# A two-layer hybrid decoder trunk: small matmuls on one pool of four PSUM banks, and another order of the first weights

## The chip, the cores and the metric

One core of a Trainium2 chip. The metric is the device time of one execution in microseconds, as the median of several runs; lower is better.

## What is computed

256 positions of width 1024 pass through two layers. A layer first runs three token mixers beside each other on one combined projection, merges them by gates, projects and adds; then it runs a SwiGLU feed-forward part. All arrays are float32.

```python
for l in range(DEPTH):                                   # 2
    h = _rmsnorm(x, mix_norm[l])
    proj = (h @ w_in[l]).astype(jnp.float32)             # 1024 x 5892
    ret_c, fox_c, rwkv_c, gate_c = jnp.split(proj, splits, axis=-1)
    y_ret = _retention_branch(ret_c, ...)                # 4 heads of 64, masked scores
    y_fox = _fox_branch(fox_c, ...)                      # 4 heads of 64, softmax with forget gates
    y_rwkv = _rwkv7_branch(rwkv_c, ...)                  # 4 heads of 64, recurrent state
    gates = jax.nn.sigmoid(gate_c).reshape(B, S, 3, D)
    merged = (gates[:, :, 0] * (y_ret @ p_ret[l]) + gates[:, :, 1] * (y_fox @ p_fox[l])
              + gates[:, :, 2] * (y_rwkv @ p_rwkv[l]))
    x = x + merged @ w_out[l]
    h = _rmsnorm(x, ffn_norm[l])
    g, u = jnp.split(h @ w_gate_up[l], 2, axis=-1)       # 2 x 2816
    x = x + (jax.nn.silu(g) * u) @ w_down[l]
```

## The kernel before

**Large products.** Activations lie transposed, features on the partitions, as eight tiles of 128 by 256. Every float32 operand of a large product is split into a high and a low part of type fp32r, and a product is three matmuls: high by high, then the two mixed ones (`mm3`, line 300). Weights come by DMA as pieces of 1 MB into three `raw` buffers, ACT casts the high part of eight tiles (line 287), DVE subtracts for the low part (288); four such pairs (`whi`, `wlo`) are buffered, and `refill` (294) keeps up to three cast pieces ahead. The products of one pair of output tiles collect in one PSUM bank of the tag "mm" (four banks). `gemm_n` (489) makes the columns of fox and ret that are needed with the positions on the partitions.

**Small products.** The mixers use about a thousand matmul records with few rows, columns or both. RWKV's go to two PSUM banks of the tag "rw", those of fox, ret and the norms to two of the tag "fr". Many address a part of the array: 64 rows by 128 columns (`pgm` 807, `psc` 1183, one head of a pair in each half of the rows), 128 by 64 (`pyf` 1123, `pyr` 1191, `pU` 947, the first part of `py` 972), 64 by 64 (`pn` 887 and 894, `pm` 859, `par` 935, `pS` 957, the second part of `py` 980), 32 by 32 (`px` 906 and 914) and 128 by 8 (`pc` 1061, the running sums of the forget gates). Transposes (`ptr` 842, `pqk`, `px` 1113, `pv` 998) use the whole array. `pb` (793) is the bonus product of RWKV; DVE reads it for `bon` (795). In `fox` the causal mask is added by a bf16 product of an identity with the mask, behind the diagonal block's scores (1101).

**Order.** `mixers` (539) runs generators: the large products ("gemm") and the chains of RWKV, fox and ret. Each `yield` gives a cost from the table `PACE`, and the generator whose clock is lowest goes next; where the merge needs a branch (`self.need`), that one runs to its end first. This gives every instruction a rank, and the framework's scheduler then orders each engine's instructions by rank and by estimated times of readiness, allots buffers and sets the waits. On the chip each engine keeps that order.

**The start.** 22 products of zeros run first (`pz`, 172 to 176). The first weight tile `w[0]` is fetched in three pieces: columns 0 to 511 on ACT's queue, 512 to 1023 and 1024 to 2047 on SP's queue, which also fetches x, the parameters and the next tiles, in the order of lines 183 to 191. `first_pairs` (345) goes over the contraction in four steps of two feature tiles, and in each over four pairs of outputs; a pair and step has four weight tiles, hence twelve matmuls, tile by tile through `mm3`. In its last step come the sums of squares and `replicate` (474), which puts the inverse norm on all partitions for `rwkv_in` (672).

## Time and profile before

| | |
|---|---|
| runs | 795.17, 795.45, 798.04 us; median 795.45 |
| the profiled execution | 795.98 us, its span 794.0 us |
| TensorE (PE) | 785.9 us busy, 99% |
| VectorE (DVE) | 569.4 us, 72% |
| ScalarE (ACT) | 403.6 us, 51% |
| GpSimd (POOL) | 15.0 us, 2% |
| DMA | 140.42 MB, mean 177 GB/s |
| granted clock of TensorE | 1.0 |

The span runs from the first to the last instruction of the profiled execution; its own time has 2.0 us more. All stretches are in microseconds from the span's start. Layer 0's mixers lie between about 31 and 185 us, its feed-forward part ends near 410, and layer 1 follows in the same shape. PE is matmul and PEld the weight load that overlaps it; a matmul record lasts longer than the distance to the next one, since matmuls are pipelined. One float32 matmul of the program leaves two records.

### The profile page before, as it was taken

The numbers are of one execution on the slowest core, as the hardware profiler recorded it, in microseconds if no ns is written. First come the engines' busy times: TensorE is split into PE (matmuls) and PEld (weight loads), VectorE is DVE, ScalarE is ACT, GpSimd is POOL, SyncE is SP. The second block draws the span as 40 slices with busy tenths as digits, with TensorE's granted clock in tenths as the row PEclk, the third lists the DMA queues.
The fourth block names the chain that finished last, engine by engine and source line by source line (L and its number), as shares of the span: only waits on it lengthen the run. The fifth ranks groups of instructions, "written<-read, shape, count | busy, mean of one in ns | idle before, by whom it ended". The sixth has DMA issues, their size and how long they took to land.

```text
span 794.0 us, 16539 instructions
## 1 busy us (share of the span) xinstructions
PE 785.9 (99%) x7010; PEld 761.8 (96%) x7010; DVE 569.4 (72%) x919; ACT 403.6 (51%) x563; POOL 15.0 (2%) x51
## 2 busy tenths in 40 slices
PE   8999999999999999999999999999999999999998
PEld 7999999999999999999998998998999999999998
DVE  5887888778866666656668798877787766666453
ACT  6577445345646544535446773544356544444331
POOL 3000000000000000000020000000000000000000
PEclk9999999999999999999999999999999999999999
DMA  8755434425555555555564453442355465564650
GB/s 319 259 173 181 152 118 167 133 74 220 192 193 201 178 206 193 171 195 199 199 203 174 174 173 111 167 166 81 134 213 211 161 213 176 196 210 162 208 192 27
DMA packets 28234, 140.42 MB, mean 177 GB/s; under 512 B 7648, under 2 KB 9216, under 8 KB 13184
## 3 DMA queue, kind: packets, MB, share of 16 engines
q1 hardware_dynamic: 28016, 139.10, 50.5%
q8 instruction: 55, 0.90, 0.5%
q10 hardware_dynamic: 144, 0.26, 0.1%
q14 instruction: 19, 0.16, 0.1%
HBM read 136.97 MB, written 1.33 MB: 174 GB/s over the span
## 4 chain that ended last, share of the span: by engine, by line
PE 94%; DVE 2%; DMA 2%; ACT 1%; issue 0%; SPq 0%; DVEq 0%; ACTq 0%
PE mm L304 27%; PE mm L307 27%; PE mm L308 27%; DVE wlo L288 1%; PE mqk L487 1%; PE mqk L486 1%; PE mqk L485 1%; DMA raw<-in_win 1%; ACT whi L287 1%; PE mv L485 1%; PE pgm L807 1%; PE mv L486 1%; PE mv L487 1%; DMA rsw<-rqk 1%; PE ptr L842 1%; PE psc L1183 0%
## 5 line engine op out<-in xcount | busy, mean ns | idle before, releaser
L287 ACT CAST whi<-raw 128x1024 fp32r<-128x1024 f32 (+1 forms) x257 | 264.9, 1033 | 311.4 <-PE mm L307 220.6
L288 DVE TENSOR_TENSOR wlo<-raw,whi 128x1024 fp32r<-128x1024 f32 (+1 forms) x257 | 308.7, 1203 | 152.0 <-ACT whi L287 151.4
L304 PE MATMUL mm<-xh,whi 128*128 128x256 f32 x1312 | 367.6, 280 | 1.6 <-ACT whi L287 1.3
L308 PE MATMUL mm<-xh,wlo 128*128 128x256 f32 x1264 | 351.0, 278 | 0.1
L307 PE MATMUL mm<-xl,whi 128*128 128x256 f32 x1264 | 350.6, 277 | 0.1
L304 PEld LDWEIGHTS mm<-xh,whi 128*128 128x128 f32 x1312 | 246.6, 188 | 4.0 <-ACT whi L287 1.5
L307 PEld LDWEIGHTS mm<-xl,whi 128*128 128x128 f32 x1264 | 237.5, 188 | 1.4 <-issue 0.5
L308 PEld LDWEIGHTS mm<-xh,wlo 128*128 128x128 f32 x1264 | 237.3, 188 | 1.1 <-issue 0.3
L307 PE MATMUL mm<-lo,whi 128*128 128x256 f32 x576 | 160.2, 278 | 0.2
L308 PE MATMUL mm<-hi,wlo 128*128 128x256 f32 x576 | 160.2, 278 | 0.0
L304 PE MATMUL mm<-hi,whi 128*128 128x256 f32 x576 | 160.0, 278 | 0.0
L307 PEld LDWEIGHTS mm<-lo,whi 128*128 128x128 f32 x576 | 108.2, 188 | 1.0 <-DVE lo L425 0.6
L304 PEld LDWEIGHTS mm<-hi,whi 128*128 128x128 f32 x576 | 108.2, 188 | 0.6 <-issue 0.3
L308 PEld LDWEIGHTS mm<-hi,wlo 128*128 128x128 f32 x576 | 108.1, 188 | 0.3
L650 DVE TENSOR_TENSOR h<-t,mm 128x512 f32<-128x512 f32 x22 | 15.1, 687 | 11.3 <-PE mm L308 8.4
L647 DVE TENSOR_TENSOR t<-mm,rstd 128x512 f32<-128x512 f32 (+1 forms) x24 | 15.1, 645 | 8.5 <-PE mm L308 8.5
L485 PE MATMUL mv<-whi,xh 128*128 128x260 f32 (+1 forms) x64 | 18.7, 293 | 0.0
L487 PE MATMUL mv<-whi,xl 128*128 128x260 f32 (+1 forms) x64 | 18.4, 287 | 0.0
L588 DVE TENSOR_TENSOR gate<-mm,rstd 128x512 f32<-128x512 f32 x24 | 16.4, 684 | 2.7 <-PE mm L308 2.7
L486 PE MATMUL mv<-wlo,xh 128*128 128x260 f32 (+1 forms) x64 | 18.4, 287 | 0.0
L597 DVE SCALAR_TENSOR_TENSOR gate<-gate,mm 128x512 f32<-128x512 f32 x24 | 15.9, 678 | 2.4 <-PE mm L308 2.3
L440 ACT ACTIVATE xh<-x,par 128x256 fp32r<-128x256 f32 x32 | 14.8, 501 | 2.5 <-DVE x L661 1.7
(257 smaller groups left out, 716.5 us busy)
## 6 DMA issues: line engine op xcount, KB each, us to landing
raw<-in_wg SPq DMA_DIRECT2D x44, 1024.0 KB
raw<-in_wgate SPq DMA_DIRECT2D x24, 1024.0 KB
raw<-in_wd SPq DMA_DIRECT2D x16, 1024.0 KB
raw<-in_win SPq DMA_DIRECT2D x13, 1024.0 KB
raw<-in_wo SPq DMA_DIRECT2D x8, 1024.0 KB
raw<-in_wd SPq DMA_DIRECT2D x8, 768.0 KB
raw<-in_wqk SPq DMA_DIRECT2D x4, 1024.0 KB
raw<-in_pp SPq DMA_DIRECT2D x4, 1024.0 KB
```

Of the source, the lines that this page charges most:

```text
L287: nc.scalar.copy(hi[:, :m * width], r)
L288: nc.vector.tensor_tensor(out=lo[:, :m * width], in0=r, in1=hi[:, :m * width].bitcast(F32), op=ALU.subtract)
L304: nc.tensor.matmul(out, wh, xh, start=first, stop=False)
L307: nc.tensor.matmul(out, wh, xl, start=False, stop=False)
L308: nc.tensor.matmul(out, wl, xh, start=False, stop=last)
L485: nc.tensor.matmul(out, xh[:, s], wh, start=first, stop=False)
L486: nc.tensor.matmul(out, xh[:, s], wl, start=False, stop=False)
L487: nc.tensor.matmul(out, xl[:, s], wh, start=False, stop=last)
L588: nc.vector.tensor_tensor(out=g, in0=ps, in1=self.b2(rstd), op=ALU.mult)
L597: nc.vector.scalar_tensor_tensor(out=g, in0=g, scalar=1.0, in1=ps, op0=ALU.add, op1=ALU.mult)
L647: nc.vector.tensor_tensor(out=t[:, o, :], in0=p, in1=self.bs(rstd, o), op=ALU.mult)
L650: nc.vector.tensor_tensor(out=h, in0=t, in1=pu, op=ALU.mult)
```

## The change

- **Banks.** The tags "rw" and "fr" become one tag "sm" with four banks (`SM`); "mm" keeps four. All the lines that only rename the tag are left out below.
- **The start.** The third piece of `w[0]` and the whole of `w[1]` go to ACT's queue, behind the first piece; SP keeps the rest, x's last part comes behind `w[2]`. `first_pairs` takes four weight tiles at a time and runs the four high by high products first, then the four with the low part of the weights, then those with the low part of x.
- **replicate** moves behind the first step of "gemm" in layer 0; `rstd` is handed over in a list. In layer 1 its place stays.
- **Joined groups.** In `pn` (887), both `px` (906 and 914; one shown) and `par` (935) the loop over heads or halves is reversed. The first part of `py` moves up to stand behind `pU`; the second part runs in reverse. `psc` is made for two heads at a time in two banks, with one `yield` in place of four. `pyf` and `pyr` share a new function `rows_out`, which alternates the two column halves, last operand first. `pc` gets a weight operand padded with zeros to 128 columns. The mask goes ahead of the scores, two blocks in one product.

```diff
+SM = 4
...
         nc.sync.dma_start(par[0], d["par"][0, :, 0:P_RES])
+        nc.scalar.dma_start(w[0][:, 1024:2048], d["win0"][0, :, 1024:2048])
         nc.sync.dma_start(w[0][:, 512:1024], d["win0"][0, :, 512:1024])
-        nc.sync.dma_start(w[0][:, 1024:2048], d["win0"][0, :, 1024:2048])
-        for j in range(1, 4):
-            nc.sync.dma_start(self.xt[j], d["xt"][:, 2 * j:2 * j + 2, :])
-            if j < 3:
-                nc.sync.dma_start(w[j][:, 0:2048], d["win0"][j])
+        nc.scalar.dma_start(w[1][:, 0:2048], d["win0"][1])
+        nc.sync.dma_start(self.xt[1], d["xt"][:, 2:4, :])
+        nc.sync.dma_start(self.xt[2], d["xt"][:, 4:6, :])
+        nc.sync.dma_start(w[2][:, 0:2048], d["win0"][2])
+        nc.sync.dma_start(self.xt[3], d["xt"][:, 6:8, :])
...
-        ps = [self.ps.tile([P, 2, T], F32, tag=t, bufs=n, name=self.nm("mm")) for t, n in (("rw", 2), ("rw", 2), ("mm", 4), ("mm", 4))]
+        nc = self.nc
+        ps = [self.ps.tile([P, 2, T], F32, tag=t, bufs=n, name=self.nm("mm")) for t, n in (("sm", SM), ("sm", SM), ("mm", 8 - SM), ("mm", 8 - SM))]
...
-                if kk == 3 and j == 3:
-                    rstd = self.replicate(dg)
-                for m in range(2):
-                    for k in range(2 * kk, 2 * kk + 2):
-                        if not self.cur:
-                            self.refill()
-
-                        self.mm3(ps[j][:, m, :], self.block(), xs[k], k == m == 0, k == KT - 1 and m == 1)
-        return ps, rn, rstd
+                ws = []
+                while len(ws) < 4:
+                    if not self.cur:
+                        self.refill()
+                    ws.append(self.block())
+
+                for n, (i, o) in enumerate(((0, 0), (1, 0), (0, 1))):
+                    for b in range(4):
+                        m, k = b // 2, 2 * kk + b % 2
+                        nc.tensor.matmul(ps[j][:, m, :], ws[b][i], xs[k][o], start=n == b == kk == 0, stop=n == 2 and b == 3 and kk == 3)
+        return ps, rn, dg
...
-            ps, rn, rstd = self.first_pairs(xs)
+            ps, rn, dg = self.first_pairs(xs)
...
-            rstd = self.replicate(dg)
-        rw = self.rwkv_in(l, xs, rstd, ps)
-        clock = {"gemm": 0.0, "rwkv": 0.0}
-        run = {"gemm": self.gemms(l, xs, rstd, rn), "rwkv": self.rwkv(l, rw)}
+        rstd = []
+        gemms = self.gemms(l, xs, rstd, rn)
+        clock = {"gemm": next(gemms) if l == 0 else 0.0, "rwkv": 0.0}
+        rstd.append(self.replicate(dg))
+        rw = self.rwkv_in(l, xs, rstd[0], ps)
+        run = {"gemm": gemms, "rwkv": self.rwkv(l, rw)}
...
         for p in range(NP):
-            for h in range(2):
+            for h in (1, 0):
                 nc.tensor.matmul(px[hs[h], p, :], nn[hs[h], p, :], dn[hs[h], p, :], start=True, stop=True, tile_position=(64 * h, 64 * h))
...
-        for a in range(2):
-            pa = self.ps.tile([P, NC - 1, 2 * C], F32, tag="rw", bufs=2, name=self.nm("par"))
+        for a in (1, 0):
+            pa = self.ps.tile([P, NC - 1, 2 * C], F32, tag="sm", bufs=SM, name=self.nm("par"))
...
-        pu = self.ps.tile([P, 2, NC - 1, 64], F32, tag="rw", bufs=2, name=self.nm("pU"))
+        pu = self.ps.tile([P, 2, NC - 1, 64], F32, tag="sm", bufs=SM, name=self.nm("pU"))
         for q in range(NC - 1):
             for a in range(2):
...
                     nc.tensor.matmul(pu[hs[h], a, q, :], gg[:, u, 0:C], uw[:, u, :], start=q == a == 0, stop=q == NC - 2 and a == 1,
                                      tile_position=(0, h * 64))
+
+        py = [self.ps.tile([P, 2, 2, C], F32, tag="sm", bufs=SM, name=self.nm("py")) for _ in range(2)]
+        for q2 in range(NC // 2):
+            for a in range(2):
+                for h in range(2):
+                    for e in range(2):
+                        u = unit(a, 2 * q2 + e, h)
+                        nc.tensor.matmul(py[h][hs[e], q2, a, :], gg[:, u, C:2 * C], uw[:, u, :], start=q2 == a == 0, stop=False,
+                                         tile_position=(0, e * 64))
...
-                pS = self.ps.tile([P, 64], F32, tag="rw", bufs=2, name=self.nm("pS"))
+                pS = self.ps.tile([P, 64], F32, tag="sm", bufs=SM, name=self.nm("pS"))
...
-        py = [self.ps.tile([P, 2, 2, C], F32, tag="rw", bufs=2, name=self.nm("py")) for _ in range(2)]
-        for q2 in range(NC // 2):
...
-        for q2 in range(NC // 2):
-            for a in range(2):
-                for e in range(2):
+        for q2 in (1, 0):
+            for a in (1, 0):
+                for e in (1, 0):
                     for h in range(2):
                         q = 2 * q2 + e
                         if q:
                             nc.tensor.matmul(py[h][hs[e], q2, a, :], ar[hs[h], a, q, C:], S[a][q - 1][hs[h], :], start=False,
-                                             stop=q2 == NC // 2 - 1 and a == 1, tile_position=(64 * h, e * 64))
+                                             stop=q2 == 1 - e and a == 0, tile_position=(64 * h, e * 64))
...
-        pt = lambda n, shape: self.ps.tile(shape, F32, tag="fr", bufs=2, name=self.nm(n))
-
-        na, lf = sm.tile([P, 2, 4], F32, name="na"), sm.tile([P, 2, 8], F32, name="lf")
+        pt = lambda n, shape: self.ps.tile(shape, F32, tag="sm", bufs=SM, name=self.nm(n))
+
+        na, lf = sm.tile([P, 2, 4], F32, name="na"), sm.tile([P, 2, P], F32, name="lf")
+        nc.gpsimd.memset(lf[:, :, 8:], 0.0)
...
-        nc.tensor.matmul(pc[0:8, :], lf[:, 0, :], c["tri"][:, 0, :], start=True, stop=False)
-        nc.tensor.matmul(pc[0:8, P:T], lf[:, 1, :], c["tri"][:, 1, P:T], start=False, stop=True)
+        nc.tensor.matmul(pc, lf[:, 0, :], c["tri"][:, 0, :], start=True, stop=False)
+        nc.tensor.matmul(pc[:, P:T], lf[:, 1, :], c["tri"][:, 1, P:T], start=False, stop=True)
...
                 pl = pt("pl", [P, 2, T])
+
+                nc.tensor.matmul(pl[:, :, t * P:n], self.identb, self.maskb.unsqueeze(1).broadcast_to([P, 2, P]), start=True, stop=False)
                 for i in range(2):
                     h = 2 * a + i
                     for b in range(t + 1):
-                        o = pl[:, i, b * P:(b + 1) * P]
-                        nc.tensor.matmul(o, qa[:, h, t * P:(t + 1) * P], ka[:, h, b * P:(b + 1) * P], start=True, stop=b < t)
-                        if b == t:
-                            nc.tensor.matmul(o, self.identb, self.maskb, start=False, stop=True)
+                        nc.tensor.matmul(pl[:, i, b * P:(b + 1) * P], qa[:, h, t * P:n], ka[:, h, b * P:(b + 1) * P],
+                                         start=False, stop=i == 1 and b == t)
...
-        for h in range(4):
-            a, s = h // 2, slice((h % 2) * 64, (h % 2) * 64 + 64)
-            vs = slice(h * 64, h * 64 + 64)
-            nc.tensor.matmul(py[s, a, 0:P], v[:, 0, vs], pT0[:, h, 0:P], start=True, stop=True)
-            nc.tensor.matmul(py[s, a, P:T], v[:, 0, vs], pT0[:, h, P:T], start=True, stop=False)
-            nc.tensor.matmul(py[s, a, P:T], v[:, 1, vs], pT1[:, h, :], start=False, stop=True)
+        self.rows_out(py, lambda t, h: v[:, t, h * 64:h * 64 + 64], pT0, pT1)
         self.dbg("fox", l, py)
         self.y[1] = self.split(self.t2, py, [P, 2, T], ("t2", "t2"))
+
+    def rows_out(self, py, v, p0, p1):
+
+        for a in (1, 0):
+            for first, t, q, p in ((True, 1, slice(P, T), p1), (False, 0, slice(P, T), p0), (True, 0, slice(0, P), p0)):
+                for i in (1, 0):
+                    h = 2 * a + i
+                    self.nc.tensor.matmul(py[i * 64:i * 64 + 64, a, q], v(t, h), p[:, h, :] if t else p[:, h, q], start=first,
+                                          stop=not first or q.start == 0)
...
-        for h in range(4):
-            a, s = h // 2, slice((h % 2) * 64, (h % 2) * 64 + 64)
-            ps = self.ps.tile([P, 384], F32, tag="fr", bufs=2, name=self.nm("psc"))
-            nc.tensor.matmul(ps[:, 0:T], qk[s, 2 + a, 0:P], qk[s, a, :], start=True, stop=True)
-            nc.tensor.matmul(ps[:, T:], qk[s, 2 + a, P:T], qk[s, a, P:T], start=True, stop=True)
-            nc.vector.tensor_tensor(out=sc[:, h, :], in0=ps[:, 0:T], in1=rmask[:, h, :], op=ALU.mult)
-            nc.vector.tensor_tensor(out=sc1[:, h, :], in0=ps[:, T:], in1=rmask[:, h, 0:P], op=ALU.mult)
-            yield PACE["ret1"]
-        py = self.ps.tile([P, 2, T], F32, tag="fr", bufs=2, name=self.nm("pyr"))
-        for h in range(4):
-            a, s = h // 2, slice((h % 2) * 64, (h % 2) * 64 + 64)
-            nc.tensor.matmul(py[s, a, 0:P], v[:, 0, h, :], sc[:, h, 0:P], start=True, stop=True)
-            nc.tensor.matmul(py[s, a, P:T], v[:, 0, h, :], sc[:, h, P:T], start=True, stop=False)
-            nc.tensor.matmul(py[s, a, P:T], v[:, 1, h, :], sc1[:, h, :], start=False, stop=True)
+        for a in range(2):
+            ps = [self.ps.tile([P, 384], F32, tag="sm", bufs=SM, name=self.nm("psc")) for _ in range(2)]
+            for t in range(2):
+                for i in range(2):
+                    s = slice(i * 64, i * 64 + 64)
+                    nc.tensor.matmul(ps[i][:, t * T:T + t * P], qk[s, 2 + a, t * P:(t + 1) * P], qk[s, a, t * P:], start=True, stop=True)
+            for i in range(2):
+                h = 2 * a + i
+                nc.vector.tensor_tensor(out=sc[:, h, :], in0=ps[i][:, 0:T], in1=rmask[:, h, :], op=ALU.mult)
+                nc.vector.tensor_tensor(out=sc1[:, h, :], in0=ps[i][:, T:], in1=rmask[:, h, 0:P], op=ALU.mult)
+        yield PACE["ret1"]
+        py = self.ps.tile([P, 2, T], F32, tag="sm", bufs=SM, name=self.nm("pyr"))
+        self.rows_out(py, lambda t, h: v[:, t, h, :], sc, sc1)
```

## Rows read from the trace of the kernel before

**Rows 1.** The page's head: span, busy time by engine, chain that ended last by engine.
```profile
span 794.0 us, 16539 instructions
...
PE 785.9 (99%) x7010; PEld 761.8 (96%) x7010; DVE 569.4 (72%) x919; ACT 403.6 (51%) x563; POOL 15.0 (2%) x51
...
PE 94%; DVE 2%; DMA 2%; ACT 1%; issue 0%; SPq 0%; DVEq 0%; ACTq 0%
```

**Rows 2.** Busy time by stretch: length, then PE, PEld, DVE, ACT, POOL, clock, DMA.
```profile
91.27:107.05 15.78, 15.75 (x142) 13.50 (x141) 13.56 (x23) 3.27 (x5) 0.00 (x0) 1.00 0.29 105
...
235.40:410.30 174.90, 174.90 (x1538) 174.87 (x1537) 110.20 (x122) 85.80 (x102) 4.29 (x12) 1.00 0.55 191
```

**Rows 3.** Timeline of PE: start, length, line, operation, tiles, shapes, matmuls merged.
```profile
91.06 0.28 PE L308 MATMUL mm<-xh,wlo 128*128 128x256 f32 x1
91.27 1.16 PE L807 MATMUL pgm<-rav,bk 64*128 64x128 f32 x8
92.35 0.39 PE L304 MATMUL mm<-xh,whi 128*128 128x256 f32 x1
92.57 0.28 PE L307 MATMUL mm<-xl,whi 128*128 128x256 f32 x1
...
101.57 0.94 PE L807 MATMUL pgm<-rav,bk 64*128 64x128 f32 x14
102.35 0.41 PE L1183 MATMUL psc<-rqk 64*128 64x256 f32 x1
```

**Rows 4.** Timelines of PE and DVE: the product pb and its reader.
```profile
83.56 1.02 PE L793 MATMUL pb<-rkk,con 128*128 128x512 f32 x2
...
98.95 0.68 DVE L795 TENSOR_TENSOR bon<-v,pb 128x512 f32<-128x512 f32 x1
```

**Rows 5.** Timeline of PE: first and last row of ptr and pyr in turn.
```profile
104.59 0.99 PE L842 MATMUL ptr<-con,rav 128*128 128x128 f32 x6
...
106.83 0.39 PE L308 MATMUL mm<-xh,wlo 128*128 128x256 f32 x1
```

**Rows 6.** Timeline of PE: two records of a group ahead of the rest.
```profile
145.84 0.33 PE L887 MATMUL pn<-dn,nn 64*64 64x64 f32 x2 [0.15 <-DVE dn L882]
146.09 0.39 PE L304 MATMUL mm<-hi,whi 128*128 128x256 f32 x1
...
153.71 0.21 PE L906 MATMUL px<-t,gg 32*32 32x32 f32 x2
153.85 0.39 PE L308 MATMUL mm<-hi,wlo 128*128 128x256 f32 x1
```

**Rows 7.** Timeline of PE: py begins, large products after it, pv.
```profile
168.31 0.69 PE L972 MATMUL py<-uw,gg 128*64 128x64 f32 x16
...
170.64 0.38 PE L304 MATMUL mm<-xh,whi 128*128 128x256 f32 x1
...
179.03 0.60 PE L998 MATMUL pv<-con,ysq 128*128 128x128 f32 x4
```

**Rows 8.** Timeline of PE: pc and the second large matmul behind it.
```profile
62.19 0.60 PE L1061 MATMUL pc<-con,lf 128*8 128x256 f32 x2
...
63.16 0.28 PE L307 MATMUL mm<-xl,whi 128*128 128x256 f32 x1
```

**Rows 9.** Timeline of the start, PE and ACT; in brackets the wait and its releaser.
```profile
6.23 0.58 PE L304 MATMUL mm<-xh,whi 128*128 128x256 f32 x1 [0.31 <-ACT xh L440]
...
7.28 0.28 PE L304 MATMUL mm<-xh,whi 128*128 128x256 f32 x1
...
8.22 0.62 ACT L287 CAST whi<-raw 128x512 fp32r<-128x512 f32 x1 [1.64 <-DMA raw<-in_win]
...
8.89 0.39 PE L304 MATMUL mm<-xh,whi 128*128 128x256 f32 x1 [1.33 <-ACT whi L287]
```

**Rows 10.** Busy time by stretch, columns as in rows 2; DMA share and GB/s end the line.
```profile
3.50:6.00 2.50, 2.43 (x12) 1.39 (x10) 0.36 (x2) 0.85 (x2) 1.77 (x6) 1.00 0.74 178
...
8.00:10.00 2.00, 1.11 (x9) 1.11 (x10) 0.69 (x1) 1.13 (x2) 0.00 (x0) 1.00 1.00 419
```

More of the change, by code (lines that the diff above doesn't have):

```diff
@@ L322, in gemm_halves @@
     def gemm_halves(self, xs, kcut=None, hook=None, tag="mm"):
-        ps = [self.ps.tile([P, T], F32, tag=tag, bufs=4 if tag == "mm" else 2, name=self.nm("mm")) for _ in range(2)]
+        ps = [self.ps.tile([P, T], F32, tag=tag, bufs=8 - SM if tag == "mm" else SM, name=self.nm("mm")) for _ in range(2)]
         n = len(xs) if kcut is None else KT
@@ L489, in gemm_n @@
     def gemm_n(self, width, xs, name="mv"):
-        ps = [self.ps.tile([P, width], F32, tag="mm", name=self.nm(name)) for _ in range(2)]
+        ps = [self.ps.tile([P, width], F32, tag="mm", bufs=8 - SM, name=self.nm(name)) for _ in range(2)]
         for k in range(KT):
@@ L543, in mixers @@
         if l == 0:
-            ps, rn, rstd = self.first_pairs(xs)
+            ps, rn, dg = self.first_pairs(xs)
         else:
-            ps = [self.gemm_halves(xs, 7, tag="rw"), self.run(self.gemm_pair(xs))]
+            ps = [self.gemm_halves(xs, 7, tag="sm"), self.run(self.gemm_pair(xs))]
             rn, dg = self.rstd()
             ps.append(self.run(self.gemm_pair(xs)))
-            rstd = self.replicate(dg)
-        rw = self.rwkv_in(l, xs, rstd, ps)
-        clock = {"gemm": 0.0, "rwkv": 0.0}
-        run = {"gemm": self.gemms(l, xs, rstd, rn), "rwkv": self.rwkv(l, rw)}
+        rstd = []
[4 more added lines that the diff above has]
+        run = {"gemm": gemms, "rwkv": self.rwkv(l, rw)}
         self.start = []
@@ L578, in gemms @@
         rt = []
-        for _ in self.ret_in(l, xs, rstd, rn, rt):
+        for _ in self.ret_in(l, xs, rstd[0], rn, rt):
             yield PACE["gemms1"]
@@ L587, in gate @@
             g = gates[b, c] = self.big.tile([P, 2, T], F32, tag="gate", bufs=8, name=self.nm("gate"))
-            nc.vector.tensor_tensor(out=g, in0=ps, in1=self.b2(rstd), op=ALU.mult)
+            nc.vector.tensor_tensor(out=g, in0=ps, in1=self.b2(rstd[0]), op=ALU.mult)
             nc.scalar.activation(g, g, AF.Tanh, scale=0.5)
@@ L801, in rwkv @@
         for a in range(2):
-            pg2 = [self.ps.tile([P, NC, 2 * C], F32, tag="rw", bufs=2, name=self.nm("pgm")) for _ in range(2)]
+            pg2 = [self.ps.tile([P, NC, 2 * C], F32, tag="sm", bufs=SM, name=self.nm("pgm")) for _ in range(2)]
             for q in range(NC):
@@ L838, in rwkv @@
             for a in range(2):
-                ptr = self.ps.tile([P, 2 * NC, 64], F32, tag="rw", bufs=2, name=self.nm("ptr"))
+                ptr = self.ps.tile([P, 2 * NC, 64], F32, tag="sm", bufs=SM, name=self.nm("ptr"))
                 for q in range(NC):
@@ L902, in rwkv @@
         v1 = self.t2.tile([P, NP, B], F32, tag="t2", name=self.nm("v1"))
-        px = self.ps.tile([P, NP, B], F32, tag="rw", bufs=2, name=self.nm("px1"))
+        px = self.ps.tile([P, NP, B], F32, tag="sm", bufs=SM, name=self.nm("px1"))
         for p in range(NP):
-            for h in range(2):
+            for h in (1, 0):
                 nc.tensor.matmul(px[hi[h], p, :], gg[lo[h], 2 * p + h, 2 * C + B:], t1[lo[h], p, :], start=True, stop=True,
@@ L910, in rwkv @@
         yield PACE["rwkv22"]
-        px = self.ps.tile([P, NP, B], F32, tag="rw", bufs=2, name=self.nm("px2"))
+        px = self.ps.tile([P, NP, B], F32, tag="sm", bufs=SM, name=self.nm("px2"))
         for p in range(NP):
-            for h in range(2):
+            for h in (1, 0):
                 nc.tensor.matmul(px[lo[h], p, :], v1[hi[h], p, :], tb[hi[h], p, h, B:], start=True, stop=True,
@@ L964, in rwkv @@
             yield PACE["rwkv17"]
-        py = [self.ps.tile([P, 2, 2, C], F32, tag="rw", bufs=2, name=self.nm("py")) for _ in range(2)]
-        for q2 in range(NC // 2):
-            for a in range(2):
-                for h in range(2):
-                    for e in range(2):
-                        u = unit(a, 2 * q2 + e, h)
-                        nc.tensor.matmul(py[h][hs[e], q2, a, :], gg[:, u, C:2 * C], uw[:, u, :], start=q2 == a == 0, stop=False,
-                                         tile_position=(0, e * 64))
-        for q2 in range(NC // 2):
-            for a in range(2):
-                for e in range(2):
+        for q2 in (1, 0):
+            for a in (1, 0):
+                for e in (1, 0):
                     for h in range(2):
```

28 lines of the change are left out of this document (14 added, 14 removed).

## The prediction

> **What bounds the kernel now.** I read the head of the page first: TensorE is busy 99% of a span of 794.0 us, and it makes up 94% of the chain of work that ended last [rows 1]. So the time is the sum of what TensorE does one thing after another, and an edit counts by the TensorE time that it takes out or puts in. Because matmuls overlap in the records, I price by the distance from start to start and not by the duration column. The table of stretches gives the steady price: in the long feed-forward stretch 1538 matmuls take 174.90 us, 0.114 us each [rows 2]. The same table shows the dense part of the mixers, 91.27 to 107.05 us, where only 142 matmuls start or run in 15.78 us [rows 2]. I then read that part in the timeline to see what a visit of small matmuls costs. A large matmul before a visit takes 0.21 us (91.06 to 91.27) and the one after it 0.22 (92.35 to 92.57) in place of 0.114 [rows 3]: about 0.10 lost going in and 0.11 coming out. Inside, eight records of pgm take 1.08 us. At 101.57, fourteen of the same shape take 0.78, or 0.056 each [rows 3]; there the two heads alternate and run side by side, in the first visit one head runs alone. (One float32 product leaves two records, as pc does [rows 8].) The cause is a bank: pb is written at 83.56 and holds one of the two "rw" banks until DVE reads it at 98.95 [rows 4].
>
> **The cluster from 91.27 to 107.05.** By the code 104 of the 142 records are small: 32 pgm, 16 psc, 24 pyf, 24 pyr, 8 ptr. The other 38 at 0.114 take 4.3 us, so the small ones and their edges take 11.5 [rows 2]. With four banks pgm's heads can alternate, psc is written in pairs of heads, and pyf and pyr alternate two column halves; 32 + 24 + 24 records of 128 columns at 0.056 are 4.5 us, psc's eight of 256 and eight of 128 columns are 1.3, and ptr's eight at twice 0.056, alone, 0.9: together 6.7. I allow five visits at 0.4 (0.10 in, 0.11 out, and the 0.18 by which eight lone records exceed eight times 0.112 [rows 3]). That makes 8.7, and **2.8 us less per layer**. The stretch from 104.59 to 106.83 shows what goes: ptr and the rest of pyr change places four times in 2.24 us [rows 5], for 8 records at 0.112 and 6 at 0.056, 1.2 us. pyr now starts with the product whose operand is written last, so nothing is left to hold its rest back.
>
> **Split groups.** At 145.84 two records of pn take 0.25 us by themselves, with the other thirty of the 32 behind large matmuls; at 153.71 two of px take 0.14 [rows 6]. Each such early pair costs itself, less some 0.05 of streaming that remains, and 0.21 for the two edges: 0.41 and 0.30. The pattern stands four times per layer: pn (line 887), px (906), px again (914), and par (935), cut in two halves. Reversing the order of the heads (or of a) puts the product with the latest operand first. With 0.30 for the second px and 0.41 for par that is **1.4 us per layer**.
>
> **py and pU.** From 168.31 to 170.64 py's two tilings alternate in four runs [rows 7]. Now the 32 records with 128 rows stand behind pU, which has their tiling, and the rest are one run: three inner changes at 0.1, **0.3 us per layer**.
>
> **pc.** Two products with an output of eight partitions and one large matmul take 0.97 us, with 0.10 before them [rows 8]. As full-array products they stream 2 × 0.224 + 2 × 0.112 = 0.67, and with an exit of 0.1 and the large matmul they take 0.88: **0.2 per layer**. The wider operand costs a memset on GpSimd, which is 2% busy [rows 1].
>
> **The mask products, the banks' names, replicate later.** The mask's four products of 128 columns become two of 256: the same columns. Fewer changes of type could give 0.2 per layer, an early bank held by the mask could take as much; I count zero. That rstd is now computed behind the first step of the large products costs nothing as long as these fill TensorE, as they do; without that cover it would be one product and one ACT copy, under 1 us.
>
> **The start.** The first weight piece gives twelve products. TensorE begins them at 6.23, starts the fourth at 7.28 and the next only at 8.89, after waiting 1.33 us for ACT's cast of the second piece, which lands at 8.22 [rows 9]: the compiled order has put a product of the second piece ahead of eight that are left of the first. With the high parts of four tiles first, none of the first products needs the late low part of x, and all twelve can run before the piece: eight at 0.114 are **0.9 us**. What the two queues do to that piece no row shows. From 3.5 to 6 us the DMA engines are 74% busy at 178 GB/s, from 8 to 10 fully at 419 [rows 10], so there is idle capacity and the third piece on ACT's queue could use it: at best the second lands a microsecond sooner (gain 1.9). At worst the third piece, 0.52 MB, goes through beside it: 1.25 us at 419 GB/s, and the gain turns into a loss of 0.3. I take 0.9, the piece landing when it does now, since one gap and one load offset each other. The small parameter transfer, which the first products need, may lose some tenths by sharing, inside these ends. Three more issues on ACT's queue fall in time when ACT has nothing to cast.
>
> The Trainium skill speaks against this part: "DMA: Bandwidth & Descriptors", section "Issuing engines are not separate DMA queues", says that transfers issued by different engines run on the same 16 DMA engines and interleave, so a second queue saves only issue time. By it alone the start would gain no bandwidth; the 74% above says that some was left unused. No run here yet shows two queues for longer than one transfer.
>
> **The sum.** 2 × (2.8 + 1.4 + 0.3 + 0.2) + 0.9 = 10.3 us. The profiled execution took 795.98 us around its span of 794.0, so 785.7; the median of the runs before is 795.45, 0.5 lower, and I say **785.5**.
>
> **The rivals.**
> A. The groups don't stay whole. The order on TensorE is made by a scheduler from estimated times, and a shared pool lets three chains mix more finely: banks held by pb, psc and pgm together are already four, so a half group or an early pair can come back elsewhere. For it speaks the start, where that order was wrong by 1.33 us [rows 9]; against it, that with the latest operand first there is nothing to split off. Half of the 9.4 would be left: 790.
> B. DVE becomes the bound. In the cluster it is busy 13.56 of 15.78 us [rows 2], more than the 13.0 that my sum leaves. Against it, the weights are cast some pieces ahead, and DVE is at 72% over the span [rows 1]. If the cluster gains nothing, 785.5 + 5.6 = 791.
> C. Slower: a bank held in the shared pool blocks a chain that had its own pair. Today pb's bank is held 15.4 us [rows 4], and fox and ret pay nothing for it. If such a hold makes the RWKV chain late by 15 us per layer, the large matmuls that now stand between py and pv, 8.4 us from 170.64 to 179.03 [rows 7], run out first and TensorE waits the other 7: 785.5 + 14 = 799.5. It decides from about 13 us of delay; with two banks more in reach I see no such hold that four banks don't shorten.
> D. The second queue delays the second weight piece by the 1.25 us above, the other steps holding: 0.9 becomes -0.3, 786.7. This is where the rule of "DMA: Bandwidth & Descriptors" (the Trainium skill) would lead. The full 419 GB/s after 6 us [rows 10] is for it, the idle share before 6 us against it.
>
> **How the numbers follow.** Forecast 0.52, A 0.22, B 0.07, C 0.07, D 0.12. About 0.5%, 4 us, is what a measurement of this kernel can tell from no change. Forecast and D lie beyond it (0.64, less a few hundredths), A straddles it (0.13 beyond, 0.09 within), B is mostly within: faster 0.78, same 0.14, slower 0.08. The low end takes the best of each term: cluster 3.9 with two visits fewer and fewer lone records, splits 1.7 with the waits that precede some of them, 0.5 and 0.3, start 1.9, together 14.7, 780.5; I give 780. The high end takes in A and B, 792, and leaves out C.
>
> **What would show it.** Right: pgm in one or two visits at 0.056 per record; pn, px and par with no early pair; pyr uncut; pU and the first part of py in one visit; no stall near 7.3 us, and the second cast at about 8.2. Wrong in A's way: the same records with as many visits. B: TensorE idle with DVE named as releaser. C: large idle times before the merges. D: the second cast after 9 us. The forecast is wrong if the span falls by less than 5 us, or if it falls while the cluster stays as long.

## The result, and the profile after

The changed kernel takes 789.93 us (median of 4 runs, 788.77 to 790.28) against 796.54 for the kernel before (4 runs): ratio 0.9914, 95% interval 0.9889 to 0.9939, 6.6 us less between the medians, 0.86% by the ratio. A second set of runs gave 789.38 against 795.96, ratio 0.9914 (0.9900 to 0.9928). The forecast of 785.5 had the sign and the range right and asked for a gain of 10.3 us. In the two profiles the spans differ by 5.6 us. So the question is where some 4 us of the expected gain went.

The page after, lines of its head and its chain line; they answer to [rows 1].

```profile
span 788.4 us, 16505 instructions
...
PE 773.3 (98%) x7002; PEld 754.3 (96%) x7002; DVE 569.8 (72%) x919; ACT 405.1 (51%) x563; POOL 16.8 (2%) x53
...
PE 89%; DVE 4%; DMA 3%; ACT 2%; issue 1%; SPq 1%; DVEq 0%; ACTq 0%
```

TensorE's share of the chain fell from 94% to 89%: waits have moved onto the path. The view of PE's waits names them (who waited, for whom, us in total, times, longest; three rows are left out).

```profile
PE pn L894 <- DVE dn L889: 2.5, 2, 2.2
PE mm L368 <- ACT whi L289: 1.6, 2, 1.1
PE mm L368 <- ACT xh L445: 1.3, 1, 1.3
...
PE mm L306 <- DVE fn L1032: 0.8, 1, 0.8
PE pv L1006 <- DVE ysq L999: 0.7, 2, 0.4
PE px L1122 <- DVE lg L1118: 0.7, 2, 0.3
PE pg L737 <- DVE sg L720: 0.7, 1, 0.7
...
PE mm L368 <- DVE wlo L290: 0.5, 1, 0.5
...
```

Lines 289, 290, 368 and 445 belong to the start, 720 and 1032 to layer 0's beginning, behind the moved `replicate`; 889, 999 and 1118 come in both layers. The cluster is what the prediction asked for; the timeline of PE in layer 0, answering to [rows 3, 4, 5]:

```profile
99.43 1.58 PE L1198 MATMUL psc<-rqk 64*128 64x256 f32 x16
101.06 1.12 PE L800 MATMUL pb<-rkk,con 128*128 128x512 f32 x2
...
102.94 1.53 PE L1139 MATMUL pyr<-rsc,rv 128*64 128x128 f32 x24
104.30 1.48 PE L1139 MATMUL pyf<-pT,fv 128*64 128x128 f32 x24
105.71 2.63 PE L814 MATMUL pgm<-rav,bk 64*128 64x128 f32 x32
108.27 1.09 PE L849 MATMUL ptr<-con,rav 128*128 128x128 f32 x8
```

Each group stands whole, in one visit. To see each term of the sum I take the length of a stretch from the first product of one group to the first of another, less 0.114 us for every large product inside. The stretches of the changed kernel (view of windows, tile mm alone: start and end, length, PE's busy time and the count of large products, granted clock, DMA share, GB/s): first layer 0's cluster, then `pm` to `pu` (it begins with the first large product behind `pm`), `pu` to `pU`, `pU` to behind `pv`, then layer 1's `pm` to `pu`.

```profile
88.88:109.12 20.24, 11.02 (x88) 1.00 0.41 151
135.72:159.75 24.03, 20.12 (x164) 1.00 0.37 125
159.75:164.61 4.86, 1.31 (x9) 1.00 0.58 216
164.61:177.74 13.13, 9.30 (x70) 1.00 0.15 45
...
521.60:547.05 25.45, 19.97 (x164) 1.00 0.34 118
```

The same stretches before:

```profile
83.56:106.82 23.26, 11.41 (x85) 1.00 0.32 112
136.56:158.10 21.54, 17.67 (x137) 1.00 0.47 156
158.10:162.51 4.41, 1.00 (x5) 1.00 0.01 4
162.51:179.38 16.87, 12.89 (x100) 1.00 0.28 94
```

(In the first and third row of before, two large products only lap over an edge: 83 and 3 count.) So the cluster costs 23.26 - 83 x 0.114 = 13.8 before and 20.24 - 88 x 0.114 = 10.2 after. All stretches worked out so, in us:

| stretch | term | forecast per layer | layer 0 | layer 1 |
|---|---|---|---|---|
| cluster, from its first small product | cluster | -2.8 | -3.6 | -3.8 |
| `pm` to `pU` | split groups | -1.4 | -0.8 | +0.5 |
| `pU` to `pv` | py and pU | -0.3 | -0.3 | -0.3 |
| `pc` to `pnk` | pc | -0.2 | -0.1 | -0.2 |
| `pnk` to the cluster, cluster to `pm` | mask; nothing | 0 | +0.4 | +0.5 |
| `pw` to `pc` | replicate | 0 | +1.6 | -0.4 |
| sum | | -4.7 | -2.8 | -3.7 |
| start, up to the sums of squares (26.86 before, 27.82 after) | start | -0.9 (once) | +1.0 | |

The cluster gave 1.8 us more than forecast; the start, `replicate` and the split groups fell short by 5.6, and the stretches forecast at nothing cost 0.9. One entry depends on the execution that was profiled: the +0.5 of layer 1's split groups holds a wait of 2.18 us for `dn`. In a second profile of the same kernel that wait is 1.00, and the two entries of the row are -0.6 and -0.7.

### The profile page after: what moved, and what is told of

The parts are those of the page before. It is cut to its first block, busy times and chain, and to the rows that moved or that the text cites. A ratio compares the mean times of both kernels' runs of the same rounds, so it can differ in the third digit from the quotient of the medians.

```text
span 788.4 us, 16505 instructions
## 1 busy us (share of the span) xinstructions
PE 773.3 (98%) x7002; PEld 754.3 (96%) x7002; DVE 569.8 (72%) x919; ACT 405.1 (51%) x563; POOL 16.8 (2%) x53
## 3 DMA queue, kind: packets, MB, share of 16 engines
HBM read 136.97 MB, written 1.33 MB: 175 GB/s over the span
## 4 chain that ended last, share of the span: by engine, by line
PE 89%; DVE 4%; DMA 3%; ACT 2%; issue 1%; SPq 1%; DVEq 0%; ACTq 0%
PE mm L310 25%; PE mm L306 25%; PE mm L309 25%; PE mm L368 2%; DVE wlo L290 2%; DMA d<-ti 1%; ACT whi L289 1%; DMA x<-in_xt 1%; PE mv L490 1%; PE mv L492 1%; PE mv L491 1%; PE pl L1109 1%; DMA tb<-d 1%; PE mqk L492 1%; PE mqk L490 1%
## 5 line engine op out<-in xcount | busy, mean ns | idle before, releaser
L306 PE MATMUL mm<-xh,whi 128*128 128x256 f32 x1248 | 347.9, 279 | 0.8 <-DVE fn L1032 0.8
L309 PE MATMUL mm<-xl,whi 128*128 128x256 f32 x1200 | 333.7, 278 | 0.0
L310 PE MATMUL mm<-xh,wlo 128*128 128x256 f32 x1200 | 333.5, 278 | 0.0
L306 PEld LDWEIGHTS mm<-xh,whi 128*128 128x128 f32 x1248 | 234.5, 188 | 1.2 <-issue 0.9
L309 PEld LDWEIGHTS mm<-xl,whi 128*128 128x128 f32 x1200 | 225.5, 188 | 0.8 <-issue 0.5
L310 PEld LDWEIGHTS mm<-xh,wlo 128*128 128x128 f32 x1200 | 225.3, 188 | 0.9 <-issue 0.5
L596 ACT ACTIVATE gate<-gate 128x512 f32<-128x512 f32 x24 | 15.1, 630 | 6.0 <-DVE gate L595 6.0
```

Of the source, the lines that this page charges most:

```text
L306: nc.tensor.matmul(out, wh, xh, start=first, stop=False)
L309: nc.tensor.matmul(out, wh, xl, start=False, stop=False)
L310: nc.tensor.matmul(out, wl, xh, start=False, stop=last)
L596: nc.scalar.activation(g, g, AF.Tanh, scale=0.5)
```

## The experiments

Times are medians with the ratio to the kernel before, run on the same chip in the same set (796.89, 795.41 and 795.96 us in the three sets, each on a chip of its own; across sets only ratios are compared, and a difference of ratios is given in us of 796). "Start" is where the sums of squares `pn` stand in the profile. In the expectations that place is quoted on a scale that lies up to 0.2 us off the page's.

### The start: the queues or the order

**Queues of before, blocks of four kept.**

```diff
...
-        nc.scalar.dma_start(w[0][:, 1024:2048], d["win0"][0, :, 1024:2048])
...
-        nc.scalar.dma_start(w[1][:, 0:2048], d["win0"][1])
...
+        nc.sync.dma_start(w[0][:, 1024:2048], d["win0"][0, :, 1024:2048])
+        for j in range(1, 4):
+            nc.sync.dma_start(self.xt[j], d["xt"][:, 2 * j:2 * j + 2, :])
+            if j < 3:
+                nc.sync.dma_start(w[j][:, 0:2048], d["win0"][j])
```

The two transfers on ACT's queue go back to SP's, and x's parts and the tiles come in the order of before.

> The changed kernel with the first weights on the queues and in the order of before (only the first piece on ACT's queue, all else on SP's); the blocks of four tiles stay. Theory Q (two queues share the same 16 DMA engines, so the second and third pieces, x's second part and the whole next tile land side by side and each of them late): the second piece lands near 8.2 again instead of 8.8, the PE waits of the start (whi 1.6, wlo 0.5 in the changed kernel) shrink to under 1.5 together, and the sums of squares pn (27.76 us in the changed kernel, 26.86 before) stand at 25.9 to 26.9; 1 to 1.8 us faster than the changed kernel. Theory O (the blocks of four, which ask for all four tiles' high parts at once and for two x tiles, are what waits): pn stays at 27.5 or later and the time at that of the changed kernel.

789.53 us, 0.9900 (0.9882 to 0.9918); start at 26.49. ACT's timeline, first the changed kernel, then this one: the second cast of 512 columns is the second piece, the bracket what it waited for.

```profile
8.79 0.62 ACT L289 CAST whi<-raw 128x512 fp32r<-128x512 f32 x1 [2.04 <-DMA raw<-in_win]
10.36 0.51 ACT L445 ACTIVATE xh<-x,par 128x256 fp32r<-128x256 f32 x1 [0.95 <-DMA x<-in_xt]
10.78 1.98 ACT L289 CAST whi<-raw 128x1024 fp32r<-128x1024 f32 x2
```

```profile
7.15 0.62 ACT L288 CAST whi<-raw 128x512 fp32r<-128x512 f32 x1 [0.81 <-DMA raw<-in_win]
9.19 1.05 ACT L288 CAST whi<-raw 128x1024 fp32r<-128x1024 f32 x1 [1.42 <-DMA raw<-in_win]
10.14 0.91 ACT L444 ACTIVATE xh<-x,par 128x256 fp32r<-128x256 f32 x2
```

With two queues the wanted piece is cast 1.64 us later, and the third piece 1.59 later (10.78 against 9.19). Against the kernel before, which cast the second piece at 8.22 with these same queues [rows 9], it is 0.57; the last section comes back to this. From 3.5 to 6 us the changed kernel moves 357 GB/s with the DMA engines full:

```profile
3.50:6.00 2.50, 1.66 (x12) 1.05 (x10) 0.18 (x2) 0.67 (x2) 1.55 (x4) 1.00 1.02 357
```

against 0.74 and 178 GB/s in [rows 10]. More bytes flow early, and they are the wrong ones: the whole next tile, issued on ACT's queue at 1.66 us, runs beside the piece that PE wants. From 4.5 us to the cast at 8.8 the changed kernel's view of DMA counts 1.43 MB on ACT's queue and 0.34 MB on SP's, where that piece is. Theory Q holds for the places and the waits. Its 1 to 1.8 us are not shown in the times: the ratios differ by 1.1 us and their intervals overlap, for a reason told under the clock below.

**Tile by tile, two queues kept** (`first_pairs` calls `mm3` for each tile, as before).

> The changed kernel with first_pairs tile by tile again, as before; the two queues stay. Theory Q: the pieces land as in the changed kernel, so pn stays at 27.3 to 28.3 and the time within 0.6 us of the changed kernel. Theory O: pn goes back to 26.9 or less, and the kernel is 0.9 us or more faster than the changed kernel.

789.51 us, 0.9907 (0.9893 to 0.9921); start at 28.39, second piece cast at 9.19. As theory Q has it: the order is not what waits. (In this profile the granted clock stood at 0.50 from about 7.1 to 10.4 us; as PE then still waited 0.76 us at 13.43 for a low part of the weights, little of that is left in the start.) In the seven profiles with two queues the start stands at 27.8 to 28.4 and the second piece is cast at 8.8 to 9.7.

### replicate

```diff
-        clock = {"gemm": next(gemms) if l == 0 else 0.0, "rwkv": 0.0}
-        rstd.append(self.replicate(dg))
+        clock = {"gemm": 0.0, "rwkv": 0.0}
```

with the call back in the last step of `first_pairs`.

> The changed kernel with replicate back inside first_pairs and without the first step of the large products ahead of it. Theory R (in layer 0 the move makes the RWKV inputs late, so pg waits 0.7 us for sg and a large product 0.8 us for fn): both waits fall under 0.2 us, the place of pc (64.55 in the changed kernel) comes 1 to 1.5 us earlier, the time 1 to 1.5 us less than the changed kernel. Rival (the waits belong to DVE's load there and are only moved): pc within 0.5 us of 64.55, another wait in its place, and the time unchanged.

787.92 us, 0.9888 (0.9870 to 0.9906), by the ratios 2.1 us under the changed kernel where 1 to 1.5 were expected. The waits for `sg` and `fn` are gone from the view of waits, and `pc` stands 35.3 us behind the sums of squares instead of 36.8. This is theory R. `replicate` moved back by 2.3 us (its product `pss` stands at 32.96, in the changed kernel at 35.27), and with it everything that needs `rstd`: PE had no shortage of large products, but the next visit of the RWKV chain stood in its fixed place and waited.

### The two that helped, together

> The changed kernel with both of the edits that helped, if the looks at them alone hold: the first weights on the queues of before, and replicate in its old place; blocks of four and all the rest as changed. If the two are independent, the sums of squares stand near 26.7 us (queues alone: 26.70) and pc 1.5 us nearer to them: 36.97 us behind them alone on the queues of before, 35.3 to 35.5 here; the median is 2 to 3 us under that of the changed kernel, 787 to 788. Rival (the two share a cause, or the gain is spread by the wait for dn in layer 1, which ranged from 1.0 to 2.7 us in the profiles so far): within 1 us of the changed kernel.

785.81 us, 0.9880 (0.9867 to 0.9894); start at 25.54, `pc` 35.1 us behind it. The two add up: 1.1 and 2.1 us by the ratios alone, 2.7 together. This is the time that the forecast gave to the changed kernel, and all the joined groups are still in it. In the start there is also the unexplained earlier landing of the second piece (cast at 6.89).

### The cluster: the pool or the loops

**The pool alone** (the kernel before, both tags renamed to one with four banks).

> The kernel before with nothing changed but the tags: one pool of four PSUM banks for all small products. In the order that PE is given, the stretches of one kind fall from 186 to 164 (the changed kernel has 142), and pgm is whole. Theory A (the pool alone joins the cluster around pgm; the loops rewritten by hand add the rest): 3 to 5 us faster than before, 791.5 to 793.5, pgm in one visit of some 2.6 us per layer, while pn, px and px stay split. Theory B (the gain of the change is in the rewritten loops, and the pool only lets them stand together): within 1 us of before. Theory C (a shared pool holds banks longer and makes the RWKV chain late): slower than before, with PE waits for an operand of the chain that sum to over 2 us.

794.42 us, 0.9969 (0.9957 to 0.9980). **The loops of fox and ret as before, pool and the rest as changed.**

> The changed kernel with psc, pyf and pyr in the loops of before (four yields, no alternation of halves), in the pool of four banks. In the order for PE psc stands in three pieces around pb, pyf and pgm again. Theory J (what the cluster gained comes from these loops: psc 3.26, pyf 2.82, pyr 2.72 us for both layers, against 6.18, 3.46 and 3.57 in the kernel with the pool alone): 4 to 5.5 us slower than the changed kernel, psc near 6 and pyf and pyr near 3.5. Theory P (the pool makes the gain): under 1.5 us slower.

791.87 us, 0.9958 (0.9946 to 0.9971). **Two pools of two banks, loops as changed** (`pS` on the second pool).

> The changed kernel with two pools of two banks each again (RWKV's on one, all others and pS on the other); loops, start and order of the code stay as changed. In the order for PE there are 174 stretches in place of 142, pgm in four visits of 4. Theory P (pairs need both banks of a group free at once, and in two pools they aren't: the pool carries the cluster): 4 to 6 us slower than the changed kernel, pgm back at 6 us or more for both layers (5.13 in the changed, 6.62 before). Theory J (the loops carry it): under 2 us slower. Theory C (the shared pool itself makes the RWKV chain late and costs waits): the gaps before pn fall under 0.5 us each, and the kernel is no slower than the changed kernel.

792.53 us, 0.9968 (0.9955 to 0.9980). By the same measure as in the table the cluster costs 13.8 before, 12.0 with the pool alone, 12.2 with the pool and the old loops, 12.5 with the new loops in two pools, and 10.2 with both. (Where the cluster starts with `px`, a wait of 0.35 for `lg` stands just ahead of it and counts in the row "`pnk` to the cluster"; in two pools a like wait of 0.41 stands inside the 12.5.) So neither theory holds by itself: the pool saves 1.8 per layer, the loops 1.3, both 3.6. The times lie between the theories too: the pool alone gives 2.5 us where A asked for 3 to 5 and B for 1 at most; against the changed kernel the old loops cost 3.5 (J: 4 to 5.5; P: under 1.5) and the two pools 4.3 (P: 4 to 6). In two pools a wait for `fn` of 2.2 us in layer 0 comes on top of the cluster, so its time is not the pool's alone. Theory C falls by the times: neither the kernel with the pool alone is slower than before, nor the one with two pools as fast as the changed kernel, though there the waits for `dn` fell to 0.33 in both layers, as C had it. A small trace of C remains in the cluster: `pgm` stops 0.3 us per layer in mid-group, until DVE has read `pyf`, and costs 2.6 us where 16 pairs at the 0.112 of a paired visit would be 1.8.

### The split groups

```diff
-            for h in (1, 0):
+            for h in range(2):
```

in `pn` and both `px`, and `for a in range(2)` in `par`.

> The changed kernel with the loops over heads and halves in pn, both px and par as before; the pool, the start and the rest stay as changed. In the order for PE the 8 groups of the two layers split again (first matmul alone, then large products, then the rest), 12 more stretches. Theory S (each split costs its two edges, some 0.35 us, as forecast: 1.4 per layer): waits for dn stay about as large in sum, and the kernel is 2.0 to 2.8 us slower than the changed kernel (behind the sums of squares 758.5 to 759.3 us of span against 756.5 in the changed one). Theory W (the whole pn pays with its wait for the second half of dn what the edges save; a split pn has large products between the halves that cover it): the gaps before pn, 0.62 and 2.46 us in the changed kernel, fall by 1.5 or more in sum, and the kernel is within 1 us of the changed kernel.

789.14 us, 0.9922 (0.9908 to 0.9935), against 0.9914: the joining of these four groups brings nothing that can be measured, as theory W had it. (The 756.5 us behind the sums of squares that the expectation gives to the changed kernel stand in neither of its profiles; they have 760.6 and 759.6, this one 759.0.) The stretches, `pm` to `pu`, `pu` to `pU` and `pU` to behind `pv`:

```profile
136.36:161.13 24.77, 20.82 (x163) 1.00 0.36 123
161.13:165.55 4.42, 0.86 (x3) 1.00 0.62 232
165.55:178.07 12.52, 9.32 (x75) 1.00 0.14 46
```

From `pm` to `pU` they cost 6.2 + 4.1 = 10.3, where the changed kernel has 9.2 in layer 0 (9.4 in its second profile): the edges are worth about 1 us. Behind, `pU` to `pv` costs 12.52 - 75 x 0.114 = 4.0 against 5.1: there the running sums `pS` come in two visits, not three, and `pv` finds `ysq` ready, which gives the 1 us back. That the split of `par` does this is not shown: with fox's and ret's loops as before `par` is whole, and that stretch has two visits and costs 4.1 as well. And the whole `pn` waits. DVE in layer 1 of the changed kernel, and the product that waits for it:

```profile
534.70 0.70 DVE L889 STREAM_TRANSPOSE dn<-tb 64x512 f32<-64x512 f32 x1 [1.78 <-DMA tb<-d]
535.33 0.64 DVE L604 SCALAR_TENSOR_TENSOR gate<-gate,mm 128x512 f32<-128x512 f32 x1
535.91 1.20 DVE L290 TENSOR_TENSOR wlo<-raw,whi 128x1024 fp32r<-128x1024 f32 x1
537.14 0.71 DVE L889 STREAM_TRANSPOSE dn<-tb 64x512 f32<-64x512 f32 x1
```

```profile
537.90 1.15 PE L894 MATMUL pn<-dn,nn 64*64 64x64 f32 x32 [2.18 <-DVE dn L889]
```

From the one half of `dn` to the other DVE takes 2.44 us, with a gate and a low part of weights between. Before, 19 large products (2.2 us) stood between the two parts of `pn` and covered that. But this is the smaller part of the 2.18 us. In layer 0 the halves lie as far apart, and there PE waits 0.34:

```profile
146.97 0.70 DVE L889 STREAM_TRANSPOSE dn<-tb 64x512 f32<-64x512 f32 x1
...
149.41 0.71 DVE L889 STREAM_TRANSPOSE dn<-tb 64x512 f32<-64x512 f32 x1
```

What layer 1 has on top is the 1.78 us that DVE waits for the DMA of `tb` (the bracket above). SP issues it in eight parts; in layer 0 they take 3.65 us, in layer 1 4.99:

```profile
143.81 3.65 SPq L884 DMA_DIRECT2D tb<-d  x8
529.81 4.99 SPq L884 DMA_DIRECT2D tb<-d  x8
```

Why one of the issues is late is not shown. In layer 1 it is late in all eight profiles with `pn` whole and pool and loops as changed (4.4 to 5.2 us for the eight parts), and in neither of the two with `pn` split (3.6), so the order that joining makes may bring it about. In the ten profiles with `pn` whole PE waits 0.32 to 0.57 us for `dn` in layer 0 and 0.33 to 2.44 in layer 1. So whether the small waits of the kernel with the four groups split (under 0.15 and 0.35) are all due to the cover stays open.

**pn alone split again**, on top of the kernel with queues and `replicate` as before.

> The kernel with the start's queues and replicate as before, now with the first pn in the order of before (head 0 first), so that it splits again with 19 large products between; both px and par stay joined. Theory W (a whole pn waits for the second half of dn: 0.85 and 1.10 us of gap in the profile of that kernel, up to 2.7 in others; the split has cover): gaps before pn under 0.65 in both layers, and 0 to 1.5 us faster, with less spread between runs. Theory S (each split costs its edges, 0.35 us per layer): 0.5 to 1 us slower.

785.83 us, 0.9871 (0.9854 to 0.9887) against 0.9880. The waits for `dn` fall from 1.4 to 0.25 us in sum and two stretches more come in their place; `pm` to `pu` gets 0.1 us shorter per layer. That is what theory W asked for, at the low end of its 0 to 1.5 us and within the noise: the wait and the edges weigh about the same.

### Once more, and a better start

> The changed kernel once more, unaltered, on the same chip as the three kernels below. Two causes so far for its spread of 788.8 to 790.3 us: the wait for dn in layer 1 (1.0 to 2.7 us in the profiles) and stretches at the lower clock level behind idle time of PE (in the kernel with the pool alone the granted clock was 0.50 from 9 to 12 us, behind an idle 1.3 us). Expected: 788.5 to 790.5, ratio to before 0.990 to 0.993, the sums of squares at 27.7 to 28.3 us.

789.38 us (789.04 to 789.78), as expected.

**Tile by tile on the old queues**, so that nothing of the start is changed.

> The kernel with the start's queues and replicate as before (785.8 us), now with first_pairs tile by tile as before too, so that nothing of the start is changed but the pool. Theory B (the blocks of four, high parts first, fill the time until the low parts and the third piece are there: the start gains from them once the queues are right): the wait for the second piece is back at 1.3 us or more, the sums of squares stand at 26.8 us or later, 1 to 3.5 us slower, the larger figure where the clock falls to its lower level behind the wait. Rival (the blocks are worth nothing, all of the gain was the queues): within 0.5 us of 785.8.

786.51 us, 0.9878 (0.9862 to 0.9895); start at 26.71 against 25.54. The ratios (0.9878 against 0.9880) give the blocks of four nothing. The profiles give them 1.2 us against this one kernel, but the same start stands at 26.49 and 25.78 in two others, so they show between 0.2 and 1.2. The second piece did not come late here (cast at 7.13), so the wait that theory B put back is absent; that half of it went untested. What the blocks are worth beside a piece that lands at 8.2, as in the forecast, no run shows.

**The third piece in two halves.**

```diff
...
+        nc.sync.dma_start(w[0][:, 1024:1536], d["win0"][0, :, 1024:1536])
+        nc.sync.dma_start(w[0][:, 1536:2048], d["win0"][0, :, 1536:2048])
...
```

> The kernel with the start's queues and replicate as before, with the third piece of the first weight tile fetched and cast in two halves of 256 KB. In its profile PE stood 0.80 us at 10.27 for the high part of the third piece and 0.53 us for its low part. Theory L (the piece's landing and the cast of 1.05 us in one lump set these two waits): both fall to under 0.4 us, the sums of squares come 0.5 to 1.0 us earlier than 25.87, and the median 0.5 to 1.0 us under 785.8. Rival (the bytes set it: 16 DMA engines are full from 6 us on, so the waits move to the next step's pieces): unchanged within 0.3 us.

785.30 us (784.12 to 785.68), 0.9860 (0.9844 to 0.9877); start at 26.23. The waits at the third piece are gone, and a wait of 0.6 us for a weight cast and 0.3 for a low part stand at 13.0, at the next tile. The rival holds for the waits, which moved, and the start came no earlier; PE also began with a wait of 1.13 us for `xh` there. The ratio is the lowest of all, but its interval overlaps that of the kernel without the halves (0.9880), so the halves are not shown to help. Against the changed kernel on the same chip this one is 4.1 us faster, and no run of the one reaches a run of the other. Without the halves it is 2.7 us by the ratios, and the intervals (0.9867 to 0.9894, 0.9900 to 0.9928) don't meet: the version to keep is the changed kernel with the first weights on the old queues and `replicate` in its old place.

## Why the prediction came out as it did

- **The cluster** held in its mechanism, and gave more than forecast: -3.6 and -3.8 for -2.8. The forecast allowed five visits; there are two, `psc` with `pb` and then `pyr`, `pyf`, `pgm` and `ptr`. That outweighs `pgm`, which costs 2.56 us, 0.080 per record and not the 0.056 that was to be a sign of being right. Rival A didn't come: every group that I saw whole in the code is whole in the trace.
- **The start** failed, and by its sign. The step was "the piece landing when it does now". It is cast at 8.79 (8.22 in [rows 9]), and its end of the range, a loss of 0.3, was too near: the start lost 1.0. I had bounded the loss by the third piece's 0.52 MB alone; 1.43 MB went through ACT's queue from 4.5 to 8.8 us, the next tile among them. Rival D was right in its kind (its sign, a cast after 9 us, stands in six of the seven profiles with two queues), and its price three times too small. The trace has two more issues on ACT's queue, not three. The Trainium skill, "DMA: Bandwidth & Descriptors", section "Issuing engines are not separate DMA queues", says that transfers from several engines run on the same 16 DMA engines and interleave. The trace agrees on the interleaving (both queues moved bytes from 4.5 to 8.8 us; 8.79 against 7.15 for the same piece). That a second queue saves issue time alone is not what these rows show: the rate from 3.5 to 6 us doubled, though the transfers in it were of other sizes too, and no run here separates the two.
- **replicate** at nothing failed: +1.6 in layer 0. "As long as these fill TensorE" looked at PE's supply of large products; the order is fixed, so a late operand stops PE however many large products stand behind the waiting one. I had named as price "under 1 us", one product and one copy; the price was the two waits, 1.5 us.
- **Split groups** at -1.4 per layer came to -0.8 and +0.5 in one profile and -0.6 and -0.7 in the other, and the whole of it goes when the stretch behind is counted. The edges were priced about right (1 us for 1.4). What failed is that the sum put the wait of a whole group at nothing: the split was also cover for the second half of `dn`, worth 0.3 to 0.6 us in layer 0. The rest of the 2.18 us in layer 1 comes with a late DMA that no term of the forecast held.
- **py and pU, pc** held to a tenth. **The mask** held at zero: the stretch with it, `pnk` to the cluster, is 0.2 us longer per layer, but it now ends in the wait of 0.35 for `lg`; the four score products with their mask take 1.01 us per block of two heads, 1.05 before.
- Sum: -10.3 became about -5.5 in the profiles and -6.6 in the medians. With two terms at a loss and one larger than forecast, that the time fell into the range is in part luck. (By its own working the forecast is 795.45 - 10.3 = 785.2, and the low end 780.8.)
- Rivals B and C: DVE is named in the new waits (5.4 of the 6.1 us that PE waits behind the start are on DVE, 2.5 of it for `dn`), but as the engine of a late operand, at 72% of the span as before; no idle stretch before the merges.

## What to carry to other kernels

Price an early, split piece of a group not only by its edges but by what the work between its parts covers: joining it moves that cover away, and on an engine with a fixed order one late operand stops everything behind it. Compare two profiles of the same kernel before a wait is put down to an edit: the longest one here was mostly a late DMA. When a start is limited by arrival, ask in what order the bytes arrive and not how many queues carry them; a second queue makes the wanted piece share with the next. And take an edit with several parts apart even when it is faster as a whole: two parts of this one cost 2.7 us, more than a quarter of the 9.5 that the others gave.

## What the runs showed that was not expected

**The clock behind a wait.** In the kernel with the pool alone PE waited 1.39 us for the second piece, much as in [rows 9]; two waits of 0.83 and 0.36 stood before it, and from 5 to 7 us PE was busy 0.81 us, against 1.56 in the kernel before. At about 8 us, within the wait, the granted clock fell to the lower of its two levels (0.50 is 1.2 GHz), and PE went on at it; start, length, PE busy, granted clock, DMA share and GB/s:

```profile
7.00:9.00 2.00, 0.61 (x4) 0.73 1.03 392
9.00:11.00 2.00, 2.00 (x10) 0.50 1.04 398
11.00:13.00 2.00, 2.00 (x11) 0.50 0.99 366
13.00:15.00 2.00, 2.00 (x12) 0.56 1.01 398
15.00:17.00 2.00, 2.00 (x19) 1.00 1.02 426
```

Its first 156 products took from 6.12 to 29.03 us, 2.3 us more than before. The same stands behind the wait for `dn` in layer 1 where `replicate` is back (2.44 us, to 536.20; the clock fell at about 537.9): the next group of 32, which takes 1.25 us in the changed kernel, is 1.97 long.

```profile
536.00:538.00 2.00, 1.80 (x37) 0.97 0.96 395
538.00:540.00 2.00, 2.00 (x33) 0.50 0.34 133
540.00:542.00 2.00, 2.00 (x18) 0.68 0.00 0
```

It doesn't always fall: behind 1.33 us before [rows 9] and behind 2.18 us for `dn` in the changed kernel the granted clock stayed at 1.00. In two kernels the spread between the runs goes with it. With queues as before, three runs at a mean clock of 1.000 took 787.27 to 788.92, three at 0.997 to 0.998 took 790.13 to 790.28; its profile is of the second kind, and its median, between the two, hides the better start. With `replicate` back four runs at 0.999 or 1.000 took 787.08 to 788.28, two at 0.996 and 0.997 789.86 and 790.00. In the changed kernel it does not: 788.77 and 790.28 both stand at 1.000. Which wait tips it was not tried.

**A piece that lands at two places.** With the queues of before, the second piece is cast at 8.2 in the kernel before and in the one with the pool alone, and at 6.9 to 7.2 in all five others, whose transfers up to that piece stand in the same order on the same queues, issued at the same times within 0.05 us. What differs in these five is not in the issues of the start's DMAs, and stays open.
